# A two-layer macaron decoder trunk on one core: the same instructions ordered by the scheduler with another machine model

## The chip, the cores and the metric

The kernel runs on one NeuronCore of a Trainium2 chip. The metric is the device time of one execution in microseconds (us). Five engines work side by side, each through its own queue in order: TensorE (PE, matmuls), VectorE (DVE), ScalarE (ACT), GpSimd (POOL) and SyncE (SP, which issues nearly all transfers). An instruction waits at the head of its queue until the semaphores that it needs are up, and holds everything behind it.

## The reference

```python
def reference(x, mem, ...):
    mem_n = _rmsnorm(mem, mem_norm_g)
    h = x                                            # (1, 512, 1024) float32
    for l in range(DEPTH):                           # 2 layers
        f = _swiglu(_rmsnorm(h, ffn1_pre_g[l]), ffn1_w_gate[l], ffn1_w_up[l], ffn1_w_down[l])
        h = h + 0.5 * _rmsnorm(f, ffn1_post_g[l])
        u = _rmsnorm(h, mix_pre_g[l])
        proj = u @ w_in[l]                           # q, k, v of two attentions, forget logits, q of the memory
        o_sb = _stick_breaking_attention(...)        # 8 heads of 64
        o_fx = _forgetting_attention(...)            # 8 heads of 64
        o_mem = _memory_attention(...)               # 4 heads of 128, over 256 rows of mem_n
        g_sb, g_fx, g_mem = jnp.split(jax.nn.sigmoid(u @ w_gate[l] + b_gate[l]), 3, axis=-1)
        merged = (g_sb * (_merge_heads(o_sb) @ w_br_sb[l]) + g_fx * (_merge_heads(o_fx) @ w_br_fox[l])
                  + g_mem * (_merge_heads(o_mem) @ w_br_mem[l]))
        h = h + _rmsnorm(merged @ w_out[l], mix_post_g[l])
        f = _swiglu(_rmsnorm(h, ffn2_pre_g[l]), ffn2_w_gate[l], ffn2_w_up[l], ffn2_w_down[l])
        h = h + 0.5 * _rmsnorm(f, ffn2_post_g[l])
    return h
```

`_swiglu` is `(silu(t @ w_gate) * (t @ w_up)) @ w_down` with 1024 columns in and 2816 inside.

## The kernel before

The names end in a letter and the layer: the trunk is a0 (first feed-forward of layer 0), b0 (token mixing), c0 (second feed-forward), then a1, b1, c1. The activations lie turned, 128 columns of the model by 512 tokens a tile.

**Every float32 matmul is made of three.** A weight block comes in as `raw_...` (512 KB, one transfer issued on SP, L249 or, for the blocks of the feed-forwards, L297). ACT rounds it to the high part `wh_...` (a cast, L182, or L185 with a scale), DVE subtracts that from the raw block for the low part `wl_...` (L183, or L186). Activations are split likewise (`uh`/`ul`, `us`, `ah`/`al`). `mm3` then gives PE high by high (L205), a product with one low part (L206) and one with the other (L207). Which of the two is the weight's depends on the side that it stands on: in the products of the feed-forwards L206 reads `wl` and L207 reads the low part of the activations.

**Feed-forward.** Gate and up products of the first columns are made by seven products of half size over sums of blocks (numbered 0 to 6, traced in the order 0, 2, 1, 3, 4, 5, 6; `token_product`). Tiles are named `pw` + feed-forward + `g` or `u`, the group of columns, and the sum into which the product goes. The weight sums of products 2, 3, 5 and 6 are made on DVE (L327, in tiles `t...` and `raw_...`), the activation sums too (`x11`, `x10`, `x00`, L700 to L722), and are split into `uh.._n` and `ul.._n` for product n. The results go through ACT copies and Silu (L775, L781, L786) and DVE sums (L777). The down products (`pda`, `pdc`) follow, with gate and up columns that are left over between them.

**After a product's last tile**: `result` (ACT L535 squares and sums, DVE L540 scales), `rstd` (DVE L486, ACT L483 and L488, DVE L490 and L491) and the residual (DVE L558 for the last feed-forward, then the store).

**The memory.** `mem_stats` loads the 256 rows of mem in two tiles `mstat_0` and `mstat_1` (L1022), squares and sums them on ACT (L1024) and scales on DVE (L1025). `mem_norm` makes the reciprocal root of that: ACT Ln and Exp (L1036, L1037) and four small DVE operations (L1038 to L1041). They are used late in the first feed-forward.

**The start** (`begin`) loads four tiles of x, takes their root mean squares (L535, L483, L488, L490, L491), scales and turns them (`utx`) and splits them (`us_x`).

**What sets the order.** The kernel's own planner `Q` interleaves these jobs by estimated PE times, and so sets the order in which the instructions are traced. After that the scheduler of the tile framework places each instruction in its engine's queue: it goes through the traced instructions with a model of the machine, and takes those first that this model holds ready. Some are pinned: within the start (`in_order`) and with `keep_in_program_order` they keep their traced order on their engine. The call stands in `kernel`, where the context of the framework is opened.

## Time and profile before

| | us |
|---|---|
| median of three runs | 2379.33 (2377.66 to 2384.99) |
| the profiled execution | 2378.89 |
| its span, first to last instruction | 2377.2 |
| PE busy in the span | 2348.8 |
| DVE busy | 1805.5 |
| ACT busy | 1515.2 |
| POOL busy | 76.0 |

Times in the views are counted from the start of the span. Matmuls are pipelined and drawn longer than the distance of two, so a PE that is drawn busy can still lose a little. The granted clock of TensorE is 0.999 in the mean.

### The profile page before, as it was taken

What the parts mean: (1) busy time and instruction counts of PE and PEld (TensorE: products, weight loads), DVE (VectorE), ACT (ScalarE), POOL (GpSimd) and SP (SyncE); (2) the same over time, 40 slices, a digit from 0 to 9 for tenths busy, and PEclk for the clock granted to TensorE, in tenths of its full rate; (3) what the DMA queues carried; (4) which work ended last, traced back from release to release, by engine and by line L of the source; (5) the groups of instructions that cost most, each with busy time, mean ns of one, the idle gap of its engine ahead of it and who ended that gap; (6) DMA issues with size and microseconds to landing.
All of it is one profiled execution on the core that took longest, in us unless ns stands there. A gap on an engine that the chain in (4) does not pass through costs nothing.

```text
span 2377.2 us, 31155 instructions
## 1 busy us (share of the span) xinstructions
PE 2348.8 (99%) x11719; PEld 1982.8 (83%) x11719; DVE 1805.5 (76%) x2358; ACT 1515.2 (64%) x2306; POOL 76.0 (3%) x134
## 2 busy tenths in 40 slices
PE   9999999999999999999999999999999999999998
PEld 7777889888888888778888878888888888887787
DVE  8876877667777689778788778766777767897785
ACT  6777565577766556775557665655777664666744
POOL 0000000000111000000000000000001100000000
PEclk9999999999999999999999999999999999999999
DMA  5666455223223556664647664532323235576643
GB/s 199 194 176 182 159 190 151 75 81 94 86 75 107 186 178 177 185 186 142 230 134 208 182 177 161 199 110 71 98 72 98 80 116 200 160 203 171 194 145 141
DMA packets 299754, 354.98 MB, mean 149 GB/s; under 512 B 78266, under 2 KB 192978, under 8 KB 299604
## 3 DMA queue, kind: packets, MB, share of 16 engines
q1 hardware_dynamic: 299508, 352.97, 48.3%
q8 instruction: 92, 1.51, 0.3%
q14 instruction: 58, 0.48, 0.1%
q0 software_dynamic: 96, 0.03, 0.0%
HBM read 319.39 MB, written 16.78 MB: 141 GB/s over the span
## 4 chain that ended last, share of the span: by engine, by line
PE 84%; DVE 5%; DMA 5%; ACT 4%; issue 2%; SPq 0%; POOL 0%; DVEq 0%; ACTq 0%
PE pg L206 4%; PE pg L205 4%; PE pg L207 4%; PE pda L206 2%; PE pda L207 2%; PE pdc L206 2%; PE pda L205 2%; PE pdc L207 2%; PE pdc L205 2%; PE pb L207 1%; PE pb L206 1%; PE pb L205 1%; DMA raw_da<-in_ffn_w_down_dram 1%; PE pq L206 1%; PE pq L205 1%
## 5 line engine op out<-in xcount | busy, mean ns | idle before, releaser
L205 PE MATMUL pg<-us_a,wh_wg 128*128 128x512 f32 x384 | 150.9, 393 | 0.0
L207 PE MATMUL pg<-us_a,wl_wg 128*128 128x512 f32 x384 | 149.8, 390 | 0.0
L206 PE MATMUL pg<-us_a,wh_wg 128*128 128x512 f32 x384 | 149.8, 390 | 0.0
L206 PE MATMUL pda<-wl_da,aha 128*128 128x512 f32 x224 | 87.8, 392 | 3.5 <-DVE wl_da L183 3.5
L206 PE MATMUL pdc<-wl_dc,ahc 128*128 128x512 f32 x224 | 87.9, 392 | 3.0 <-DVE wl_dc L183 3.0
L205 PE MATMUL pdc<-wh_dc,ahc 128*128 128x512 f32 x224 | 86.8, 390 | 1.4 <-ACT wh_dc L182 1.3
L205 PE MATMUL pda<-wh_da,aha 128*128 128x512 f32 x224 | 86.7, 390 | 1.1 <-ACT wh_da L182 1.1
L207 PE MATMUL pdc<-wh_dc,alc 128*128 128x512 f32 x224 | 87.2, 389 | 0.0
L207 PE MATMUL pda<-wh_da,ala 128*128 128x512 f32 x224 | 87.2, 389 | 0.0
L183 DVE TENSOR_TENSOR wl_da<-raw_da,wh_da 128x1024 fp32r<-128x1024 f32 x50 | 60.9, 1223 | 34.3 <-ACT wh_da L182 34.3
L207 PEld LDWEIGHTS pg<-us_a,wl_wg 128*128 128x128 f32 x384 | 72.1, 188 | 15.2
L183 DVE TENSOR_TENSOR wl_dc<-raw_dc,wh_dc 128x1024 fp32r<-128x1024 f32 x50 | 61.0, 1222 | 30.5 <-ACT wh_dc L182 30.4
L205 PEld LDWEIGHTS pg<-us_a,wh_wg 128*128 128x128 f32 x384 | 72.1, 188 | 14.1
L206 PEld LDWEIGHTS pg<-us_a,wh_wg 128*128 128x128 f32 x384 | 72.2, 188 | 14.1
L182 ACT CAST wh_da<-raw_da 128x1024 fp32r<-128x1024 f32 x50 | 52.2, 1050 | 47.0 <-PE pda L207 16.6
L182 ACT CAST wh_dc<-raw_dc 128x1024 fp32r<-128x1024 f32 x50 | 52.3, 1050 | 43.5 <-PE pdc L207 17.6
L186 DVE SCALAR_TENSOR_TENSOR wl_wg<-raw_wg,wh_wg 128x1024 fp32r<-128x1024 f32 x48 | 58.4, 1220 | 22.2 <-ACT wh_wg L185 22.2
L200 DVE SCALAR_TENSOR_TENSOR ga<-pg,bgate,ga 128x512 f32<-128x512 f32 x48 | 35.9, 747 | 50.0 <-ACT ga L199 50.0
L185 ACT ACTIVATE wh_wg<-raw_wg 128x1024 fp32r<-128x1024 f32 x48 | 50.6, 1058 | 24.7 <-PE pv L1096 11.7
L183 DVE TENSOR_TENSOR wl_uc<-raw_uc,wh_uc 128x1024 fp32r<-128x1024 f32 x44 | 53.7, 1220 | 16.5 <-ACT wh_uc L182 16.5
L182 ACT CAST wh_uc<-raw_uc 128x1024 fp32r<-128x1024 f32 x44 | 46.1, 1050 | 30.7 <-PE pgc L206 7.6
L183 DVE TENSOR_TENSOR wl_ua<-raw_ua,wh_ua 128x1024 fp32r<-128x1024 f32 x44 | 53.6, 1219 | 15.0 <-ACT wh_ua L182 15.0
(647 smaller groups left out, 8053.7 us busy)
## 6 DMA issues: line engine op xcount, KB each, us to landing
raw_da<-in_ffn_w_down_dram SPq DMA_DIRECT2D x66, 512.0 KB, 4.4
raw_dc<-in_ffn_w_down_dram SPq DMA_DIRECT2D x66, 512.0 KB, 4.2
raw_ga<-in_ffn_w_gate_dram SPq DMA_DIRECT2D x52, 512.0 KB, 4.3
raw_ua<-in_ffn_w_up_dram SPq DMA_DIRECT2D x52, 512.0 KB, 4.4
raw_gc<-in_ffn_w_gate_dram SPq DMA_DIRECT2D x52, 512.0 KB, 4.1
raw_uc<-in_ffn_w_up_dram SPq DMA_DIRECT2D x52, 512.0 KB, 3.6
raw_wg<-in_w_gate_dram SPq DMA_DIRECT2D x48, 512.0 KB, 3.5
raw_wo<-in_w_out_dram SPq DMA_DIRECT2D x24, 512.0 KB, 3.4
```

What stands on the lines that cost most here:

```text
L182: both = [nc.scalar.copy(h_ap, src)]
L183: make = lambda: nc.vector.tensor_tensor(l_ap, src, h_ap.bitcast(F32), ALU.subtract)
L185: both = [nc.scalar.activation(h_ap, src, AF.Copy, scale=scale)]
L186: make = lambda: nc.vector.scalar_tensor_tensor(l_ap, src, scale, h_ap.bitcast(F32), ALU.mult, ALU.subtract)
L200: nc.vector.scalar_tensor_tensor(t, z, minus, t, ALU.max, ALU.add)
L205: nc.tensor.matmul(pt, lh, rh, start=start, stop=False, skip_group_check=free)
L206: nc.tensor.matmul(pt, lh, rl, start=False, stop=False, skip_group_check=free)
L207: nc.tensor.matmul(pt, ll, rh, start=False, stop=stop, skip_group_check=free)
```

## The change

One argument is added where the context is opened:

```diff
-    with tile.TileContext(nc) as tc:
+    with tile.TileContext(nc, schedule_with_timeline_sim=True) as tc:
         tile_macaron_trunk_kernel(tc, *args)
```

The traced instructions stay the same. The scheduler now orders them with the machine model that keeps a time line, in place of the plain one. Matmuls, DVE operations and transfers are the same in number; the loads of ACT's function tables, which follow from the order, are 12 instead of 15. The queues of all engines change: on DVE and ACT about every second row stands elsewhere, on PE a fifth of the matmuls move by more than 2 us' worth of matmuls and none by more than 20. Three places:

**ACT in the start, between the third and the fourth input tile** (`us_x` is the split input, `nhx` the root mean square's small tile, `mstat_808` the first tile of the memory, `mem_rstd` its statistics; - before, + now):

```order
 L185 ACTIVATE us_x_130<-utx_0_277 128x4x128
+L185 ACTIVATE us_x_131<-utx_1_284 128x4x128
 L483 ACTIVATE nhx_114<-nhx_114,eps_t 128x1
-L185 ACTIVATE us_x_131<-utx_1_284 128x4x128
+L1024 ACTIVATE mstat_808,mem_rstd<-mstat_808 128x1024
 L488 ACTIVATE nhx_114<-nhx_114 128x1
+L1036 ACTIVATE mem_rstd<-mem_rstd 128x1
+L1037 ACTIVATE mem_rstd<-mem_rstd 128x1
 L185 ACTIVATE us_x_130<-utx_0_322 128x4x128
```

The statistics of the memory, which came after the first Silu, now stand within the root mean square of the fourth input tile. On DVE, L1025 likewise stands ahead of that tile's L490, and on SP the transfer of `mstat_0` is issued as the 13th block of 512 KB instead of the 19th. The second tile's follow ahead of `wh_ga_0_2_0`, with three table loads more than before in the first 65 us.

**PE at the start of a0's down product, the end of its up product** (`pda` is the down product, `wh_da`/`wl_da` its first weight block, `pwa0u` the up product). Before:

```order
L207 MATMUL pwa0u_1_0_1_1431<-wh_ua0_1_5_2_1544,ula0_5_665 128x512
L205 MATMUL pda0_0_0_1742<-wh_da0_0_0_0_1623,aha0_0_0_1670 128x512
L206 MATMUL pda0_0_0_1742<-wl_da0_0_0_0_1624,aha0_0_0_1670 128x512
L207 MATMUL pda0_0_0_1742<-wh_da0_0_0_0_1623,ala0_0_0_1671 128x512
L205 MATMUL pda0_0_0_1742<-wh_da0_0_0_0_1623,aha0_0_0_1670 128x512
L205 MATMUL pwa0u_1_0_0_1430<-wh_ua0_1_6_0_1583,us_x_1_131 128x512
```

Now:

```order
L207 MATMUL pwa0u_1_0_1_1431<-wh_ua0_1_5_2_1544,ula0_5_665 128x512
L205 MATMUL pda0_0_0_1742<-wh_da0_0_0_0_1623,aha0_0_0_1670 128x512
L205 MATMUL pda0_0_1_1743<-wh_da0_0_0_0_1623,aha0_0_0_1670 128x512
L205 MATMUL pwa0u_1_0_0_1430<-wh_ua0_1_6_0_1583,us_x_1_131 128x512
L206 MATMUL pwa0u_1_0_0_1430<-wl_ua0_1_6_0_1584,us_x_1_131 128x512
...
L207 MATMUL pwa0u_1_0_0_1430<-wh_ua0_1_6_2_1588,us_x_1_131 128x512
L206 MATMUL pda0_0_0_1742<-wl_da0_0_0_0_1624,aha0_0_0_1670 128x512
```

Twelve matmuls of the up product now stand between the products with `wh_da` and the first one with `wl_da`.

**PE in the gate product of c0** (`pwc0g`; the numbers behind `wh_gc0_0_` are product and row of the block; a1 and c1 change alike). Before:

```order
L207 MATMUL pwc0g_0_0_1_8095<-wh_gc0_0_3_2_8131,ulc0_3_8104 128x512
L205 MATMUL pwc0g_0_2_0_8135<-wh_gc0_0_4_0_8166,uhc0_4_8185 128x512
L206 MATMUL pwc0g_0_2_0_8135<-wl_gc0_0_4_0_8167,uhc0_4_8185 128x512
...
L207 MATMUL pwc0g_0_2_1_8136<-wh_gc0_0_4_2_8170,ulc0_4_8186 128x512
L205 MATMUL pwc0g_0_0_0_8094<-wh_gc0_0_5_0_8211,uhc0_5_8236 128x512
L206 MATMUL pwc0g_0_0_0_8094<-wl_gc0_0_5_0_8212,uhc0_5_8236 128x512
```

Now:

```order
L207 MATMUL pwc0g_0_0_1_8095<-wh_gc0_0_3_2_8131,ulc0_3_8104 128x512
L205 MATMUL pwc0g_0_0_0_8094<-wh_gc0_0_5_0_8211,uhc0_5_8236 128x512
L205 MATMUL pwc0g_0_0_1_8095<-wh_gc0_0_5_0_8211,uhc0_5_8236 128x512
L206 MATMUL pwc0g_0_0_0_8094<-wl_gc0_0_5_0_8212,uhc0_5_8236 128x512
...
L205 MATMUL pwc0g_0_2_0_8135<-wh_gc0_0_4_0_8166,uhc0_4_8185 128x512
L206 MATMUL pwc0g_0_2_0_8135<-wl_gc0_0_4_0_8167,uhc0_4_8185 128x512
```

Product 5 now begins ahead of product 4, by the 24 matmuls that product 4 has.

On DVE, ahead of the `wl` of product 5's first block, the rows of L722 and of product 4's `ul` are gone and those of product 5's `ul` and of two L327 sums for product 6 have come; in the last tiles of c1, L540 and L486 of tile 3 stand ahead of L490, L491 and L558 of tile 2.

## The prediction

> **What bounds the kernel now.** I read the page's busy shares first, then its chain of waits, then the list of what PE waited for, then stretches of the span with PE, DVE and ACT side by side.
>
> ```profile
> PE 2348.8 (99%) x11719; PEld 1982.8 (83%) x11719; DVE 1805.5 (76%) x2358; ACT 1515.2 (64%) x2306; POOL 76.0 (3%) x134
> ...
> PE 84%; DVE 5%; DMA 5%; ACT 4%; issue 2%; SPq 0%; POOL 0%; DVEq 0%; ACTq 0%
> ```
>
> ```profile
> PE pda L206 <- DVE wl_da L183: 3.5, 4, 1.3
> PE pdc L206 <- DVE wl_dc L183: 3.0, 4, 0.8
> PE pwa0u L205 <- ACT wh_ga L182: 2.0, 1, 2.0
> PE warm L1565 <- DVE warm L1656: 1.3, 1, 1.3
> PE pdc L205 <- ACT wh_dc L182: 1.3, 1, 1.3
> PE pda L205 <- ACT wh_da L182: 1.1, 1, 1.1
> PE pwa0g L207 <- DVE ula L183: 1.1, 1, 1.1
> PE pwc1u L206 <- DVE wl_uc L183: 0.8, 1, 0.8
> PE pwa0u L206 <- DVE wl_ua L183: 0.8, 1, 0.8
> PE gqx L526 <- DMA grow<-in_ffn_pre_g_dram: 0.8, 1, 0.8
> PE pwa1u L206 <- DVE wl_ua L183: 0.6, 1, 0.6
> PE pwo L206 <- DVE wl_wo L183: 0.6, 1, 0.6
> ```
>
> PE is the bound nearly everywhere, and the change neither adds nor drops a matmul, so only PE's waits can move the end. The list (engine, line, what was waited for: us in all, times, the longest; the eleven rows of 0.6 us and less behind these are left out) is short: no wait in it is longer than 2.0 us. Most are of one kind: a matmul of the low part (L206, weight wl) stands at the head of PE's queue while DVE still makes that low part.
>
> A row understates a wait. In
>
> ```profile
> 903.56 0.39 PE L207 MATMUL pwc0g<-wh_gc,ulc 128*128 128x512 f32 x1
> 903.79 0.39 PE L205 MATMUL pwc0g<-wh_gc,uhc 128*128 128x512 f32 x1
> ...
> 909.23 0.39 PE L205 MATMUL pwc0g<-wh_gc,uhc 128*128 128x512 f32 x1
> ```
>
> a matmul is drawn 0.39 us long while the next starts 0.23 later, so an idle of x in the list costs x + 0.16.
>
> **The change part by part.** Terms are added to the profiled execution's 2378.9 us, which is 0.4 below the median of the three runs, 2379.3.
>
> *1. Waits that are filled.* Wherever PE waited for a wl or a DVE result, the new order sets matmuls whose operands are long there ahead of the waiting one. At the start of the down product (second place shown above) 12 matmuls stand between the L205 and the first L206: 12 x 0.23 = 2.7 us, where the wait was at most 1.3. The waits on wh_da and wh_dc stay, since the L205 still comes straight after the same ACT cast. In the list the fillable rows are the wl ones, the wh_ga one and the ula one: 12.4 us in 14 waits, hence 12.4 + 14 x 0.16 = 14.6 us. The ula wait (1.1 + 0.16) lies in the first feed-forward's start, counted under 3. That leaves **-13.4**. Bounds: -20, if nearly the whole list went, with its small rows, and -6.7, if half of the fillers wait themselves.
>
> *2. Product 5 ahead of product 4.* In the gate product of the last three feed-forwards (third place above) PE takes product 5 before product 4, that is 24 matmuls sooner: from 909.23 to 903.79, and its first L206 from 909.46 to about 904.3. DVE makes that wl here:
>
> ```profile
> 902.59 1.21 DVE L183 TENSOR_TENSOR ulc<-x11c,uhc 128x1024 fp32r<-128x1024 f32 x1
> 903.73 1.21 DVE L327 TENSOR_TENSOR raw_gc<-tgc,raw_gc 128x1024 f32<-128x1024 f32 x1
> 904.86 1.21 DVE L183 TENSOR_TENSOR wl_gc<-raw_gc,wh_gc 128x1024 fp32r<-128x1024 f32 x1
> 900.00:920.00 20.00, 20.00 (x89) 16.26 (x88) 19.82 (x20) 11.56 (x13) 0.00 (x0) 1.00 0.68 213
> ```
>
> The third row's wl ends at 906.1, one DVE operation every 1.13 us. In the new order two of the operations ahead of it go behind (L722 and the ulc of product 4) and three come ahead (the ulc of product 5 and two L327 sums), so it ends at 906.1 + 1.13 = 907.2. PE then waits 907.2 - 904.3 = 2.9 us at its head, with product 4 ready or nearly so behind it. The last row (columns: length, PE, PEld, DVE, ACT, POOL busy, clock, DMA share, GB/s) shows DVE busy 19.82 of 20 us: nothing gives the lag back in this stretch. Three places: **+8.7**. Bounds: 0, if the lag only replaces later waits, and 10.
>
> *3. The memory statistics move to the start.* ACT's Square of mem, which stood at 36.50, now stands between L483 and L488 of the fourth input tile, and DVE's L1025 ahead of the L490 that follows:
>
> ```profile
> 22.21 0.21 ACT L488 ACTIVATE nhx<-nhx 128x1 f32<-128x1 f32 x1
> 34.23 1.28 ACT L623 ACT_TABLE_LOAD   x1
> ...
> 36.50 1.06 ACT L1024 ACTIVATE mstat<-mstat 128x1024 f32<-128x1024 f32 x1
> 37.45 0.20 ACT L1024 ACTIVATION_READ_ACCUMULATOR mstat<-mstat 128x1 f32 x1
> 77.78 0.14 DVE L1025 TENSOR_SCALAR mem_rstd<-mem_rstd 128x1 f32<-128x1 f32 x1
> ...
> 95.75 0.21 DVE L1041 TENSOR_SCALAR mem_rstd<-mem_rstd 128x1 f32<-128x1 f32 x1
> 2.00:14.00 12.00, 11.07 (x33) 5.72 (x32) 5.16 (x13) 6.82 (x15) 0.95 (x3) 1.00 0.96 331
> 30.00:90.00 60.00, 58.90 (x293) 49.68 (x293) 59.50 (x68) 42.70 (x53) 0.00 (x0) 1.00 0.42 136
> ```
>
> The chain fourth tile, turn, us_x is longer by 1.06 + 0.20 = 1.25 us. Between 30 and 90 DVE is busy 59.5 of 60 us, so there it is DVE that sets the pace, and what is put into its queue is paid in full: the ten small mem_rstd operations of which first and last are shown came at 78 to 96 and now come before 65, 10 x 0.18 = 1.8. Three more table loads before 65, 3 x 1.28 = 3.8 us, fall into ACT's 17.3 idle us and cost nothing by themselves (without that cover, 3.8). The order in the first feed-forward's products 3 and 4 makes a wl some 2.4 us late, worked out as under 2. Sum 5.45, of which some 0.5 is covered by four product matmuls now ahead of the turn: **+5**. The transfer decides the bounds: mstat_0 is now the 13th transfer of 512 KB instead of the 19th, 6.8 MB up to its end; at the 331 GB/s of the stretch from 2 to 14 it lands at about 22.6, and ACT gets there at 22.2. Bounds 1 and 9.
>
> *4. The tail.* DVE's last tile now does L540 and L486 ahead of the third tile's L490, L491 and two L558:
>
> ```profile
> 2368.33 1.41 DVE L558 SCALAR_TENSOR_TENSOR hfc<-fc,nfc,hfc 128x512 f32<-128x512 f32 x2
> 2370.65 0.69 DVE L540 SCALAR_TENSOR_TENSOR fc<-pdc,gpc 128x512 f32<-128x512 f32 x1 [0.90 <-ACT sqc L535]
> 2371.26 0.20 DVE L486 TENSOR_SCALAR nfc<-nfc 128x1 f32<-128x1 f32 x1
> 2371.96 0.22 DVE L490 SCALAR_TENSOR_TENSOR nfc<-nfc 128x1 f32<-128x1 f32 x1 [0.50 <-ACT nfc L488]
> ```
>
> So 1.41 + 0.4 us of the third tile's work, which was done before the last matmul, falls between 2371.5 and the last L490; 0.5 of it fits into the wait for ACT: **+1.3**. Bounds 0 and 1.5.
>
> *5. Token mixing.* At six places (about 588, 643, 677, 1764, 1820, 1854) a transposed weight block is split on DVE behind a weight correction that it used to precede:
>
> ```profile
> 672.61 1.67 DVE L183 TENSOR_TENSOR ptf<-ptf,ptf 128x128 fp32r<-128x128 f32 x4
> 677.24 1.23 DVE L183 TENSOR_TENSOR wl_wb<-raw_wb,wh_wb 128x1024 fp32r<-128x1024 f32 x1 [2.96 <-ACT wh_wb L182]
> 678.49 0.68 DVE L186 SCALAR_TENSOR_TENSOR q<-pq,q 64x512 fp32r<-64x512 f32 x1
> ```
>
> There the split of ptf now follows the q of 678.49, so ends after 679.3, and PE reaches the pvf product that reads it at about 678.3. Worked out so, the six are 1.0 to 1.7 us late. Before, DVE sat idle 2.96 us at this point, so it catches up; I take half, 6 x 0.7 = **+4**. Bounds 0 and 8.
>
> SP's order changes too (the next block's loads go ahead of some down weights), but there the transfers had 10 us and more in hand: nothing, and 2 to 3 us per place if that cover were gone.
>
> Sum: -13.4 + 8.7 + 5 + 1.3 + 4 = +5.6, hence 2378.9 + 5.6 = 2384.5; with the 0.4 to the median, **2385 us**.
>
> **The rivals.** *A, the fills win.* The late wl of product 5 and of the start replace waits that come behind them, as a PE that is late finds its operands ready. For it: the waits of the down products lie behind each of these places on the same chain. Against: DVE at 19.82 of 20 us. Terms 2 and 3 shrink to 2 and 1.5, and 5 to 0: -13.4 + 2 + 1.5 + 1.3 = -8.6, about 2371.
>
> *B, the transfer holds ACT and DVE.* If mstat_0 shares the bandwidth with those issued just after it, 16 transfers, 8.4 MB, must come in: at 331 GB/s it lands near 27, some 5 us after ACT gets there, and us_x, hence all of PE after its few fillers, waits; DVE, the pace-setter until 90, loses as much. From 4 us late on this alone decides. 2385 + 5 = 2390.
>
> [...]
>
> *C, the fills fail.* The fillers need weights as young as the wl that they cover; if half of them wait, term 1 is -6.7: 2385 + 6.7, about 2392. For it: in the 900 to 920 stretch DVE has no slack to make anything earlier. Against: at the down products the fillers are a product whose weights lie ready.
>
> *That the order hardly changes* is excluded: about a fifth of all matmuls move by more than 2 us.
>
> **How the numbers follow.** Forecast 2385: 0.46, with its own range from 2377 to 2392. A (2371): 0.22. B (2390): 0.14. C (2392): 0.18. A measurement of this kernel can tell about 0.3%, 7.1 us, from no change, that is below 2372 or above 2386.5. Faster: most of A, since it has the lower bounds of term 1 below it, and a little of the forecast, 0.19. Within: over half of the forecast, 0.26, with 0.05 of A and 0.04 of B and C, 0.35. Slower: the rest, 0.46. The range from 2368 to 2399 leaves out 0.1 on either side; its ends answer to about -11 and +20, where the bounds of all terms at once would give -19 and +22.
>
> **What would show it.** Right: no L206 <- wl_da or wl_dc wait, three waits of 2 to 3.4 us of a pwc0g, pwa1g and pwc1g L206 on its wl; L488 of the fourth tile at about 23.5; the last L558 ending 1.3 us further behind the last L540. Wrong: a start in which us_x is more than 3 us late (B), new PE waits of 0.5 us and more on wl inside the down products (C), or product 5 without a wait (A). A PE wait above 3.5 us anywhere, or one on a DMA, would mean that I missed a step.

## The result, and the profile after

| | before | after |
|---|---|---|
| median, us | 2382.16 (2377.66 to 2386.56, 4 runs) | 2413.60 (2411.40 to 2415.33, 4 runs) |
| the profiled execution, us | 2378.89 | 2411.40 |
| its span, us | 2377.2 | 2409.7 |
| mean granted clock of TensorE | 0.999 | 0.993 |

The ratio is 1.0136, 95% interval 1.0123 to 1.0150: the change makes the kernel 31.4 us slower. The forecast was 2385, and its range ended at 2399.

The changed kernel's page, busy time by engine and the shares of the chain of waits:

```profile
PE 2364.3 (98%) x11719; PEld 1987.6 (82%) x11719; DVE 1801.8 (75%) x2358; ACT 1508.9 (63%) x2303; POOL 82.2 (3%) x134
...
PE 87%; DVE 6%; DMA 3%; ACT 3%; issue 2%; DVEq 0%; SPq 0%; ACTq 0%
```

Same work, PE drawn 15.5 us longer, and waits between. Its list of what PE waited for (us in all, times, the longest):

```profile
PE pts L1135 <- DVE k L183: 5.7, 2, 2.8
PE pv L205 <- DVE ga L200: 2.6, 2, 1.3
...
PE pwc0g L206 <- DVE wl_gc L183: 1.6, 1, 1.6
PE pb L205 <- ACT o L182: 1.6, 2, 0.8
PE pwa1g L205 <- ACT sa L775: 1.6, 1, 1.6
PE pwc1g L205 <- ACT sc L775: 1.6, 1, 1.6
PE pwc0g L205 <- ACT sc L775: 1.6, 1, 1.6
PE pwc1g L206 <- DVE wl_gc L183: 1.6, 1, 1.6
```

The rows on `wl_da` and `wl_dc`, which headed the list before, are gone. In their place stand `pts`, `pv` and `pb`, which lie in the token mixings and had no row there at all, and at the first gate product of c0, a1 and c1 two kinds of wait.

**Where the time went.** For every PE record I took the distance to the next one, less the usual distance of its form (0.227 us for 128x512), and summed what is left by stage. It is the time that PE loses to waits and to a lower clock together; in the kernel before it is 38.6 us in all, after it is 69.9. Differences to the kernel before, in us, with four of the experiments below beside them ("gate" is the first gate chunk):

| stage | after | three places, DVE put back (e13) | mixings put back (e17) | start put back (e18) | four stretches put back (e12) |
|---|---|---|---|---|---|
| a0, the first 80 us of PE's work | +4.0 | +3.8 | +4.0 | -0.1 | +0.3 |
| a0, the next 70 us | -2.4 | -2.5 | -1.9 | -1.6 | +0.4 |
| rest of a0 | -2.8 | -2.8 | -2.8 | -1.8 | -2.9 |
| token mixing b0 | +9.9 | +9.8 | +0.9 | +9.6 | +0.6 |
| gate of c0 | +6.7 | +0.3 | +6.4 | +7.0 | 0.0 |
| rest of c0 | -0.6 | -0.5 | +2.8 | +2.6 | -1.4 |
| gate of a1 | +4.3 | +0.2 | +4.3 | +4.3 | 0.0 |
| rest of a1 | -1.6 | -1.0 | +0.4 | +2.1 | -3.3 |
| token mixing b1 | +11.6 | +11.4 | +6.6 | +11.4 | +4.7 |
| gate of c1 | +5.4 | +0.6 | +5.7 | +5.3 | 0.0 |
| rest of c1 | -3.2 | -0.5 | -1.5 | -2.6 | -4.0 |
| sum | +31.3 | +18.8 | +24.9 | +36.2 | -5.6 |

Single stages scatter by 1 to 3 us from run to run, as one half-clock stretch more or less falls on them: the rest of c0 stands at +2.8 and +2.6 with e17 and e18, which have one at 1003 and at 1009 us, and at -0.6 with the changed kernel, whose clock is 1.00 there.

**The gate of c0.** PE between product 3 and product 5 (start, drawn length, instruction, in brackets the idle time and its releaser):

```profile
912.17 0.39 PE L207 MATMUL pwc0g<-wh_gc,ulc 128*128 128x512 f32 x1
914.18 0.98 PE L205 MATMUL pwc0g<-wh_gc,uhc 128*128 128x512 f32 x2 [1.62 <-ACT sc L775]
916.81 0.79 PE L206 MATMUL pwc0g<-wl_gc,uhc 128*128 128x512 f32 x1 [1.65 <-DVE wl_gc L183]
```

Product 5 adds into the banks that hold product 3's sum, and ACT must first copy that sum out (L775). Before, the 24 matmuls of product 4, which has other banks, lay over the copy. Now PE stands for it, 1.78 us, and again for `wl`, 1.91 us. The windows behind (length, busy time of PE, PEld, DVE, ACT, POOL, then the granted clock, DMA share, GB/s):

```profile
914.00:916.00 2.00, 0.98 (x2) 0.37 (x2) 2.00 (x3) 0.61 (x2) 0.00 (x0) 1.00 0.00 0
916.00:918.00 2.00, 1.19 (x3) 1.00 (x4) 2.00 (x3) 0.08 (x1) 0.00 (x0) 0.54 0.55 153
918.00:920.00 2.00, 2.00 (x7) 1.52 (x6) 2.00 (x2) 0.97 (x1) 0.00 (x0) 0.50 0.97 314
920.00:922.00 2.00, 2.00 (x6) 1.61 (x5) 0.23 (x1) 0.47 (x1) 0.00 (x0) 0.50 0.77 226
922.00:924.00 2.00, 2.00 (x8) 1.55 (x7) 1.23 (x1) 0.57 (x1) 0.00 (x0) 0.75 1.05 386
```

The clock falls to half and stays there for 2 x (0.46 + 0.50 + 0.50 + 0.25) = 3.4 us' worth of lost clock, 6.8 us of time, in which PE issues a matmul every 0.43 us. And DVE (L722 and the last row make product 4's factor):

```profile
910.99 1.22 DVE L183 TENSOR_TENSOR ulc<-x00c,uhc 128x1024 fp32r<-128x1024 f32 x1
912.12 1.22 DVE L327 TENSOR_TENSOR tgc<-raw_gc,tgc 128x1024 f32<-128x1024 f32 x1
913.26 1.22 DVE L183 TENSOR_TENSOR wl_gc<-raw_gc,wh_gc 128x1024 fp32r<-128x1024 f32 x1
914.39 1.22 DVE L327 TENSOR_TENSOR tgc<-raw_gc,tgc 128x1024 f32<-128x1024 f32 x1
915.53 1.22 DVE L183 TENSOR_TENSOR wl_gc<-raw_gc,wh_gc 128x1024 fp32r<-128x1024 f32 x1
916.66 1.22 DVE L722 TENSOR_TENSOR x11c<-x11c,us_b 128x1024 f32<-128x1024 f32 x1
...
919.00 1.22 DVE L183 TENSOR_TENSOR ulc<-x11c,uhc 128x1024 fp32r<-128x1024 f32 x1
```

Four of the five rows above L722 (all but 913.26) belong to products 5 and 6, and two L327 sums for product 5 ran further up: six instructions of 1.14 us that the plain order has behind L722. Product 4's low part ends at 920.2 here, at 903.8 in the kernel before, where PE reaches this gate 8.6 us sooner (its first `pgc0` matmul at 856.7 instead of 865.3): against PE it is 8 us later.

**The token mixing b0.** PE, DVE and ACT around 588 us (`ts` is the stick-breaking chain of a head, `pts` its turned weights):

```profile
592.11 1.76 PE L1135 MATMUL pts<-ident,ts 128*128 128x128 f32 x7 [2.83 <-DVE k L183]
...
588.12 0.95 DVE L1173 TENSOR_TENSOR_SCAN ts<-cut,ts 128x384 f32<-128x384 f32 x1
588.99 1.20 DVE L183 TENSOR_TENSOR wl_wb<-raw_wb,wh_wb 128x1024 fp32r<-128x1024 f32 x1
590.22 0.69 DVE L186 SCALAR_TENSOR_TENSOR q<-pq,q 64x512 fp32r<-64x512 f32 x1
590.94 0.56 DVE L1174 TENSOR_TENSOR ts<-zs,ts 128x384 f32<-128x384 f32 x1
591.53 0.52 ACT L1175 ACTIVATE ts<-ts 128x384 f32<-128x384 f32 x1 [0.28 <-DVE ts L1174]
```

The list puts this wait down to `k`, which ended last, at 592.08; but the matmuls of L1135 read `ts`, and its last step on ACT (L1175) ended at 592.05, as late. Between the chain's scan and its last step on DVE stand the low part of a weight that is used later, and a `q`. In the kernel before that last L1174 ran ahead of both:

```profile
585.13 0.55 DVE L1174 TENSOR_TENSOR ts<-zs,ts 128x384 f32<-128x384 f32 x1
585.62 1.23 DVE L183 TENSOR_TENSOR wl_wb<-raw_wb,wh_wb 128x1024 fp32r<-128x1024 f32 x1
```

### The profile page after: what moved, and what is told of

It reads as the page before. It is cut to its first block, busy times and chain, and to the rows that moved or that the text cites. A ratio compares the mean times of both kernels' runs of the same rounds, so it can differ in the third digit from the quotient of the medians.

```text
span 2409.7 us, 31116 instructions
## 1 busy us (share of the span) xinstructions
PE 2364.3 (98%) x11719; PEld 1987.6 (82%) x11719; DVE 1801.8 (75%) x2358; ACT 1508.9 (63%) x2303; POOL 82.2 (3%) x134
## 4 chain that ended last, share of the span: by engine, by line
PE 87%; DVE 6%; DMA 3%; ACT 3%; issue 2%; DVEq 0%; SPq 0%; ACTq 0%
PE pg L206 4%; PE pg L205 4%; PE pg L207 3%; PE pda L205 3%; PE pda L207 3%; PE pda L206 3%; PE pdc L205 3%; PE pdc L207 2%; PE pdc L206 2%; PE pb L205 2%; PE pb L206 2%; PE pb L207 2%; PE pwo L205 1%; PE pwo L207 1%; PE pwo L206 1%
## 5 line engine op out<-in xcount | busy, mean ns | idle before, releaser
L206 PE MATMUL pg<-us_a,wh_wg 128*128 128x512 f32 x384 | 151.6, 395 | 0.0
L206 PE MATMUL pda<-wl_da,aha 128*128 128x512 f32 x224 | 87.2, 389 | 0.0
L206 PE MATMUL pdc<-wl_dc,ahc 128*128 128x512 f32 x224 | 87.1, 389 | 0.0
L205 PEld LDWEIGHTS pg<-us_a,wh_wg 128*128 128x128 f32 x384 | 72.8, 190 | 14.8
L206 PEld LDWEIGHTS pg<-us_a,wh_wg 128*128 128x128 f32 x384 | 72.7, 189 | 14.4
L182 ACT CAST wh_ua<-raw_ua 128x1024 fp32r<-128x1024 f32 x44 | 45.9, 1049 | 20.9 <-PE pwa1u L207 6.4
```

The lines of the kernel that those rows point to most:

```text
L182: both = [nc.scalar.copy(h_ap, src)]
L205: nc.tensor.matmul(pt, lh, rh, start=start, stop=False, skip_group_check=free)
L206: nc.tensor.matmul(pt, lh, rl, start=False, stop=False, skip_group_check=free)
```

## The experiments

All ratios are against the kernel before, timed beside it on the same chip, so they are to be held against the change's 1.0136.

### e1: product 4 ahead of product 5 again, on PE alone

```diff
-                        mm3(pts[e][:], h[:, kk, c], l[:, kk, c], un.h[:, k], un.l[:, k], opens and kk == 0,
+                        with (tc.issue_after(st["end", 4]) if n == 5 else nullcontext()): mm3(pts[e][:], h[:, kk, c], l[:, kk, c], un.h[:, k], un.l[:, k], opens and kk == 0,
                             ends and kk == ND // 2 - 1, free=True)
-                        yield 3 * S * PE_US
+                        st["end", n] = nc.cur_bb.bb.instructions[-1]; yield 3 * S * PE_US
```

> The changed kernel with one thing added: in every token product, product 5's matmuls are issued behind product 4's, as the plain scheduler had them; nearly all else stays where the time-line model put it. Theory A (product 5 directly behind product 3 waits for the scalar engine's copy of product 3's sum, L775, out of the banks into which it adds, then for its own wl, and the clock halves after the two waits): the waits at 912, 1256 and 2108 us go, with the half-clock stretches at 917, 1260 and 2114; the three places cost 16.4 us over the back-to-back issue, so the kernel takes 2396 to 2401 us. Theory B (the vector engine is simply late there, whichever product comes next, as the prediction had it: 2.9 us at each place): product 4 waits in place of product 5, and the time stays at 2408 to 2414 us.

Measured: 2431.88 us, ratio 1.0192 (1.0174 to 1.0210), worse than the change itself. Both theories miss it. Its waits:

```profile
PE pwc0g L205 <- ACT uhc L182: 7.0, 1, 7.0
PE pwc1g L205 <- ACT uhc L182: 6.3, 1, 6.3
PE pwa1g L205 <- ACT uha L182: 5.4, 1, 5.4
```

Product 4 is not "ready or nearly so", as the prediction had it: its factor is 5 to 7 us away, because DVE still does the later products' work first. Taking product 5 first was the better answer to a DVE order that was wrong already.

### e2: PE kept busy in the waits

```diff
+            with tc.issue_after(st["end", 3]):
+                for k in range(7+nb): nc.tensor.matmul(st["c", 2][0][:], zero[:], x[:, k % 4, 0, :], start=False, stop=False, skip_group_check=True)
```

Seven of them are held ahead of product 5's first matmul, the others (7, in a1 3) ahead of its first L206: 14 more matmuls in c0 and c1, 10 in a1.

> The changed kernel with 17 to 14 matmuls of zero weights added on TensorE at each of the three places where product 5 waits (c0, a1, c1): 7 behind product 3, and 7 (a1: 3) behind product 5's first two matmuls. They add nothing to the sums and stand in the time of the waits. Theory A (the half-clock stretches behind these waits, 2.6, 1.6 and 1.4 us lost, come from TensorE standing still in them): with the engine kept busy the granted clock stays at 1.00 at the three places, the waits themselves stay, and the kernel takes 2407 to 2410 us, 4 to 6 us less than the changed one. Theory B (the clock falls for another reason, such as the time of the program): the half-clock stretches stay and the time is 2413 to 2418 us.

Measured: 2414.61 us, ratio 1.0121 (1.0097 to 1.0144); mean clock 0.996 instead of 0.993. The same stretch of c0:

```profile
917.41 1.77 PE L1707 MATMUL pwc0g<-us_b,zero 128*128 128x512 f32 x7
919.50 0.50 PE L206 MATMUL pwc0g<-wl_gc,uhc 128*128 128x512 f32 x1 [0.31 <-DVE wl_gc L183]
...
918.00:920.00 2.00, 1.69 (x8) 1.10 (x7) 2.00 (x3) 0.00 (x0) 0.00 (x0) 1.00 0.29 40
920.00:922.00 2.00, 2.00 (x10) 1.60 (x10) 2.00 (x3) 1.05 (x1) 0.00 (x0) 1.00 0.93 318
```

On the clock theory A holds: at all three places it stays at 1.00, with product 5 waiting for `wl` as before. On the time it isn't shown: the interval takes in 4 us less as well as no change, since half-clock stretches came elsewhere instead (1011 and 2209 us).

### e3: the stick-breaking chain of one head ahead of the splits

```diff
-        both.append(make())
+        with (tc.issue_after(tsl["ts"]) if "ts" in tsl else nullcontext()): both.append(make())
...
-            nc.vector.tensor_tensor(t[:, :w], zr, t[:, :w], ALU.subtract)
+            sub = nc.vector.tensor_tensor(t[:, :w], zr, t[:, :w], ALU.subtract).ins; tsl.update({"ts": sub} if name.endswith("_2_1") else {})
```

> The changed kernel with one thing added: the stick-breaking chain of head 2_1 in both token mixings is put ahead of the splits (weight and query halves) that were traced behind it, on the vector and the scalar engine alone, until that head's sum over the values is traced. Theory A (TensorE's waits at 588 and 1784 us on pts come from the vector engine doing weight halves ahead of that chain, L1168, L1173, L1174, and the half-clock stretches behind them follow from the wait): both go, 6.2 and 5.9 us, and the kernel takes 2399 to 2404 us. Theory B (the chain is late from its start, since the products before it end late): the wait stays at 2 us or more at both places, and the time at 2409 to 2414 us.

Measured: 2415.00 us, ratio 1.0122 (1.0104 to 1.0140). The wait on `pts` fell from 3.6 to 1.5 us at both places and the half-clock stretch behind it went, 3.6 and 4.9 us by the sums over PE. But a `pv` matmul 66 us later now waited 1.5 us, with 0.2 or 0.3 behind it, and the time didn't move by more than it can be measured. The chain's place makes that wait; repairing one head hands part of it on.

### e8: the swap alone, in the kernel before

The plain scheduler, with product 4 held behind product 5 on PE in the gates of c0, a1 and c1:

```diff
+            for i in st["four"]:
+                tc.add_manual_dep(i, own[-1].name, nosync, reason="swapped")
```

> The kernel before, with its plain scheduler, and one part of the change alone: in the first gate chunk of c0, a1 and c1 product 4's matmuls are issued behind the whole of product 5. Theory A (the swap itself costs the copy's wait, the wl wait and the clock): 16 us in all, 2394 to 2400 us, with half-clock stretches behind the waits. Theory B (the prediction's price, 2.9 us for wl at each of three places and no copy to wait for): 2386 to 2392 us. Theory C (the swap is harmless and the loss has to do with the vector engine's new order): 2379 to 2384 us.

Measured: 2395.88 us, ratio 1.0041 (1.0018 to 1.0063), 9.3 us more than the kernel before on the same chip (2386.63). That difference is B's in size, though the interval is wide (4 to 15 us); in its pieces it is A's, a wait for the copy and in c0 a half-clock stretch. In c0:

```profile
904.38 0.99 PE L205 MATMUL pwc0g<-wh_gc,uhc 128*128 128x512 f32 x2 [0.58 <-ACT sc L775]
905.98 0.73 PE L206 MATMUL pwc0g<-wl_gc,uhc 128*128 128x512 f32 x2 [0.60 <-DVE wl_gc L183]
907.12 0.57 PE L207 MATMUL pwc0g<-wh_gc,ulc 128*128 128x512 f32 x1 [0.40 <-DVE ulc L183]
```

The three places cost 4.3, 2.7 and 2.7 us by the sums over PE, 9.7 in all. With DVE in the plain order the swap costs about what the prediction said, 8.7, but not for its reason: the wait for `wl` costs 0.8 and not 2.9, with 0.7 for the copy and 0.6 for `ul` beside it. The other 6.7 of the change's 16.4 are left for the other orders of DVE and ACT.

### e7: six instructions on DVE put behind L722

The corrections and splits traced behind the factor of product 4 are issued behind it in c0, a1 and c1; PE is not touched.

```diff
-                ins = nc.vector.tensor_tensor(src, a, b, ALU.subtract)
+                with (tc.issue_after(tsl["ts"]) if "ts" in tsl else nullcontext()): ins = nc.vector.tensor_tensor(src, a, b, ALU.subtract)
...
-            pair(4, s)
+            pair(4, s); tsl.update({"ts": nc.cur_bb.bb.instructions[-1]} if name != "a0" else {})
```

> The changed kernel with one edit, on the vector engine alone: in b's end to c0, in c0 to a1 and in c1 the corrections and low halves that belong to products 5 and 6 are issued behind the low half of product 4's factor (L722 and its L183), as the plain scheduler had them; on TensorE nothing is pinned, and the scheduler by itself puts product 4 ahead of product 5 again. Theory A (the swap on TensorE is only an answer to the vector engine's order: six instructions of 1.14 us for later products are issued ahead of L722, which made product 4 wait 7.2, 5.5 and 6.5 us when product 5 was held back alone): no wait over 1 us at the three places, no half-clock stretch there, 16 us less than the changed kernel, a ratio to the kernel before of 1.006 to 1.008. Theory B (the vector engine has more to do there than fits, in any order): a wait of 3 us or more moves to product 5 or 6, and the ratio stays over 1.011.

PE's order went back by itself, as expected: product 4 first, and no wait at products 4 and 5. Yet the time was 2415.14 us, ratio 1.0115 (1.0084 to 1.0147). The losses came back one product on, 5.3, 2.7 and 5.7 us, at the start of the up chunk:

```profile
928.89 0.73 PE L205 MATMUL pwc0u<-wh_uc,us_b 128*128 128x512 f32 x2 [0.83 <-ACT wh_uc L182]
931.78 0.69 PE L206 MATMUL pwc0u<-wl_uc,us_b 128*128 128x512 f32 x1 [2.15 <-DVE wl_uc L183]
...
927.10 1.22 DVE L327 TENSOR_TENSOR tuc<-tuc,raw_uc 128x1024 f32<-128x1024 f32 x1
...
929.37 1.22 DVE L327 TENSOR_TENSOR tuc<-tuc,raw_uc 128x1024 f32<-128x1024 f32 x1
930.50 1.22 DVE L183 TENSOR_TENSOR wl_uc<-raw_uc,wh_uc 128x1024 fp32r<-128x1024 f32 x1
```

It is the same fault again: two sums for up product 2 stand ahead of the `wl` of up product 0, which PE needs next. In the kernel before the `wl` comes first.

### e4: the memory statistics alone

```diff
-            nc.scalar.activation(raw[:], raw[:], AF.Square, accum_out=ss[:, 0:1])
+            tc.keep_in_program_order(nc.scalar.activation(raw[:], raw[:], AF.Square, accum_out=ss[:, 0:1]))
```

and the same for L1036.

> The changed kernel with one edit: the squares of the memory statistics (L1024) and their logarithms (L1036) are kept in the program's order, which puts them behind the start, as in the kernel before. Theory A (the prediction's third term: they cost the first token products 5 us by the table loads and by the scalar engine's time): 3.6 us less than the changed kernel, a ratio of 1.011 to 1.013, and the half-clock stretch at 63 us gone. Theory B (the start is late for another reason): the same ratio as the changed kernel, 1.0136, and the same waits at 47, 59 and 63 us.

Measured: 2420.10 us, ratio 1.0134 (1.0105 to 1.0162); the interval takes in both theories. The half-clock stretch at 63 us went, as A has it; the waits at 47 and 59 us stayed, the second half as long (1.0 us instead of 2.0). The first 80 us got 1.0 us shorter, and the next 70 us lost 5.6: a wait of 3.2 us for `wh_ga` came at 114 us, where the kernel before has one of 2.1, with a half-clock stretch behind it. The early statistics cost the start something, 1.0 of its 4.0 us, and pay it back there.

### e10, e11, e12, e13: stretches put back in the plain scheduler's order

From here on chosen engines are chained, for chosen stretches, in the order that they have in the kernel before; everything else is left to the time-line model. The lists of instruction numbers are long, the edit is short:

```diff
-        tile_macaron_trunk_kernel(tc, *args)
+        tile_macaron_trunk_kernel(tc, *args); as_before(nc, tc)
...
+    for numbers in AS_BEFORE:
+        chain = [by[f"I-{n}"] for n in numbers if f"I-{n}" in by]
+        for a, b in zip(chain, chain[1:]):
+            tc.add_manual_dep(b, a.name, nosync, reason="as_before")
```

> The changed kernel with the vector, scalar and GpSimd engines' order put back as the plain scheduler had it, in the two token mixings alone (the work that ran from 556 to 842 and from 1751 to 2037 us in the kernel before); TensorE's order is left to the scheduler. Theory A (the mixing's 21 us, of which the wait on pts is only a part, all come from the order of these engines): waits on pv, pts, pb and pvf go with their half-clock stretches, some 20 us less than the changed kernel, a ratio of 1.004 to 1.007. Theory B (part of it is due to TensorE's order or comes from outside the stretch): a ratio of 1.008 to 1.012.

e10 measured: 2411.42 us, ratio 1.0100 (1.0071 to 1.0128): B. The waits on `pts`, `pb` and `pvf` went, with the half-clock stretches behind them 16 us by the sums over PE; the one on `pv`, at the head of the stretch, stayed, and new ones came where the stretch ends: 2.4 us at `pgc0`, 3.5 at `utb1`.

> The changed kernel with the vector, scalar and GpSimd engines' order put back as the plain scheduler had it in the four stretches where the changed kernel lost (the start to 75 us, both token mixings with what leads into them and the factors of c0 and c1 behind them, and the end of c0 with a1's factor), and the memory statistics put back to where they were; the weight preparation in the chunks and in the down products stays as the time-line model ordered it. Theory A (losses and gains are separate, so that the gains of 14.8 us at the fills can be had alone): 2366 to 2374 us where the kernel before takes 2382, a ratio of 0.994 to 0.997. Theory B (the gains depend on what the time-line model did earlier, for instance on transfers started sooner): a ratio of 1.000 or more.

e11 measured: 2392.49 us, ratio 1.0022 (1.0006 to 1.0038). That is B by the number. Most of the loss is gone, and nothing gained: there are waits at the seams again, `utb` 2.6 and 1.7 us, `pwa0u` 2.2, and one of 2.9 us for `wh_ga` at 115 us, behind the memory statistics. Ahead of `utb` PE, which was left free, ran 16 matmuls of c0's gate among the last output products, so these ended later, and with them the chain that turns the last tile.

> The changed kernel with the vector engine alone put back to the plain scheduler's order, from the transposes ahead of c0's, a1's and c1's first gate chunk to the middle of their first up chunk (868 to 960, 1205 to 1310 and 2062 to 2155 us of the kernel before); scalar engine and TensorE are left to the scheduler. The run with six instructions moved showed the wait gone at product 5 and come back one chunk on, at the first product of the up chunk (2.5 to 3.3 us), where two corrections (tuc, L327) ran ahead of the low half that product needs. Theory A (each such wait is made by the vector engine doing later products' corrections before the halves needed next, so that the plain order on this engine alone is enough): no wait over 1.2 us at any of the three places or in the up chunk behind them, no half-clock stretch there, 14 to 17 us less than the changed kernel, a ratio of 1.006 to 1.008. Theory B (the vector engine is behind with its work as a whole, so any order only moves the wait on): the waits come again further on and the ratio stays at 1.011 to 1.014.

e13 measured: 2402.95 us, ratio 1.0064 (1.0046 to 1.0083): A. The three gates are back at +0.3, +0.2 and +0.6 us with nothing touched but DVE, and the largest wait in the first up chunks behind them is 0.75 us. This settles the gates.

> The changed kernel with TensorE, vector, scalar and GpSimd engines put back to the plain scheduler's order in four stretches (0 to 135, 545 to 960, 1195 to 1310 and 1740 to 2155 us of the kernel before); the rest, with most of the weight preparation at the chunks' ends and in the down products, is left to the time-line model. Theory A (losses and gains are separate, and what was left of the losses in the run before this one came from TensorE's order, which was free there, and from the ends of the stretches): 2368 to 2375 us where the kernel before takes 2382, a ratio of 0.994 to 0.997. Theory B (a place where the order changes from one model's to the other's makes a wait of its own, of 2 to 4 us): a ratio of 0.998 to 1.003.

e12 measured: 2376.54 us (2372.31 to 2379.84, 6 runs) against 2385.61, ratio 0.9955 (0.9938 to 0.9972), 9 us faster than the kernel before: A. Its longest waits:

```profile
PE pwa0u L205 <- ACT wh_ga L182: 2.5, 1, 2.5
PE pts L1135 <- ACT ts L1175: 2.5, 1, 2.5
```

The first is the old one behind the memory statistics, the second a seam at the head of b1. So losses and gains can be had apart. Whether it takes TensorE's order or other places for the seams, in which e11 differs, was not tried singly.

### e15: the fills alone

> All four engines in the plain scheduler's order but for four short stretches around the first down products of each feed-forward (185 to 240, 1020 to 1075, 1360 to 1410 and 2200 to 2245 us of the kernel before), which are left to the time-line model: the fills alone, the prediction's first term. The kernel before waits there 3.1, 3.3, 2.5 and 2.0 us. Theory A (the time-line model fills these waits by itself, whatever stands ahead): 6 to 9 us less than the kernel before, a ratio of 0.996 to 0.9975. Theory B (the fills were bought by work that it moved ahead of the stretch): a ratio of 0.999 to 1.001.

Measured: 2384.21 us, ratio 0.9994 (0.9981 to 1.0007): B. The waits at the first down products did get shorter, but others came, the largest 3.6 us for L1042, which scales the rows of mem. Fills that cost nothing elsewhere weren't to be had this way.

### e16: the vector engine's whole order

> The changed kernel with the vector engine's whole order put back to the plain scheduler's, all 2325 rows of it; TensorE, scalar, GpSimd and SyncE are left to the time-line model. Theory A (the vector engine's order makes all the losses and most of the gains; the other engines' orders follow from it): the ratio is 1.000, within 0.002, with waits at the down products' starts as in the kernel before. Theory B (TensorE's own order under this model makes waits too, as at the transposes behind the token mixings, 2.4 to 3.5 us, when vector and scalar engine were put back there alone): a ratio of 1.003 to 1.008. Theory C (the gains are TensorE's and the scalar engine's): a ratio of 0.994 to 0.997.

Measured: 2456.51 us, ratio 1.0293 (1.0266 to 1.0321): 70 us slower, outside all three theories, B's in kind. DVE has row for row the order that it has in the kernel before. Its three longest waits:

```profile
PE utb L578 <- DVE fb L568: 7.6, 2, 3.8
PE pda L205 <- ACT pda L827: 5.9, 2, 3.7
PE pts L1135 <- DVE fl L1341: 5.2, 2, 2.6
```

Over the whole program, a good order on one engine with other orders beside it was worse than a poor one that all share; in the three short stretches of e13 it was better.

### e17 and e18: a whole stretch on all four engines

> The changed kernel with all four engines put back to the plain scheduler's order from the end of a's last down product to the transposes behind the token mixing, in both layers (545 to 880 and 1740 to 2075 us of the kernel before). Put back on the vector, scalar and GpSimd engines alone, the waits on pts, pb and pvf had gone and new ones of 2.4 to 3.5 us had come at pgc0 and utb, where TensorE's order was free. Theory A (the mixing's own loss is 20 us, and a stretch put back on all engines keeps it): 17 to 21 us less than the changed kernel, a ratio of 1.005 to 1.007. Theory B (the waits at the stretch's end come with any seam between the two orders): a ratio of 1.009 to 1.012.

e17 measured: 2405.20 us, ratio 1.0078 (1.0057 to 1.0099), between the two. b0 came down to +0.9 us; b1 to +6.6, of which 4.3 are two waits at its head (`pv` 1.5, `pts` 2.8).

> The changed kernel with all four engines put back to the plain scheduler's order from the start to 135 us of the kernel before, and so with the memory statistics at 77 to 95 us again. Theory A (the prediction's third term, 5 us lost at the start): 3 to 5 us less than the changed kernel, a ratio of 1.0115 to 1.0125. Theory B (the statistics cost the same wherever they stand: the kernel before waits 2.1 us at 111 us for what they held up, and the run with the statistics moved alone showed 3.2 us at 114): the changed kernel's ratio, 1.013 to 1.014.

e18 measured: 2415.35 us, ratio 1.0119 (1.0101 to 1.0136). The start came down from +4.0 to -0.1, and 0.8 of the 2.4 gained in the 70 us behind it was given back; the interval takes in both theories, the sums of this stage speak for A. The whole sum is larger than the change's all the same (+36.2), since two half-clock stretches, at 1009 and 1354 us, fell on this execution that the changed kernel's did not have.

## Why the prediction was wrong

The direction was the one held likeliest, slower; the size was not. Of the 25.8 us between the forecast's +5.6 and the measured +31.4, term 5 holds 17.5 and term 2 holds 7.7. Behind both, the clock was put at nothing: no term has a share for it, but the trace before has a half-clock stretch behind two short waits, at 2170 us (last section).

**1, fills, -13.4: right in size.** No wait on `wl_da` or `wl_dc` is left, and the places where PE lost less sum to -14.8. But 2.2 of them, the `wh_ga` wait at 111 us, are no fill: e4 and e18 bring that wait back with the statistics. Some 1.6 more are that half-clock stretch at 2170 us, which went with the waits ahead of it and which the term did not count. And the fills don't come alone (e15).

**2, product 5 ahead of product 4, +8.7: 16.4 measured.** The step that failed is "PE then waits 907.2 - 904.3 = 2.9 us at its head, with product 4 ready or nearly so behind it". The wait for `wl` was 1.91, 0.82 and 1.84 us, less than forecast. What was left out is the wait for the copy of product 3's sum, 1.78 at each place, and the half clock behind the two, 2.6, 1.6 and 1.4 us (the clock that is lost while PE works). Under it lies a wrong reading: the swap was taken for the cause, when it was the scheduler's answer (e7: it went back by itself) to a DVE order that makes product 4's factor 8 us later. The rows for that were on the table, since L722 was seen to go behind; only product 5's `wl` was followed, not what L722 feeds. e1, e7 and e13 show it from three sides.

**3, the start, +5: +4.0, in part by luck.** L488 of the fourth tile ran at 23.93 (forecast 23.5), and the load of `mstat` was 0.98 us late for ACT:

```profile
22.87 1.06 ACT L1024 ACTIVATE mstat<-mstat 128x1024 f32<-128x1024 f32 x1 [0.98 <-DMA mstat<-in_mem_dram]
...
23.93 0.19 ACT L488 ACTIVATE nhx<-nhx 128x1 f32<-128x1 f32 x1
```

So rival B's transfer was late, but by 1 us and not 5. The sum is not made of the forecast's pieces, though: 1.6 of the 4.0 is a half-clock stretch at 63 us that the term did not have, behind waits of 1.1 us for `wh_ga` and 2.0 for `wl_ga`, and with the statistics alone put back only 1.0 went (e4). That the rest lies in the order of the start is shown by e18; in which rows is not. The term also left out the other side, 2.4 us gained in the 70 us behind it.

**4, the tail, +1.3: right.** From the last matmul to the end of the span it is 8.4 us, before 7.3; the last L558 ends 4.35 us after the last L540 starts, before 3.17.

**5, token mixing, +4: 21.5 measured, the largest miss.** The step that failed is the choice of places: they were sought by one kind of moved row, the split of `ptf` behind a weight correction, and of its six places two show a wait (`pvf`, 0.6 us each). The chain of L1168, L1173 and L1174 in front of `pts` (3.6 us at each mixing), the `ga` in front of `pv` (1.5) and the `o` in front of `pb` (1.0) moved in the same way and were not followed. "DVE sat idle 2.96 us at this point, so it catches up" held for DVE and did PE no good, since the wait comes before the idle time. That these losses lie in the mixing's own order is shown for b0 by e17 (+9.9 to +0.9) and less cleanly for b1. Which engine's order makes them was not separated: e10 chains three engines, e17 four.

**The rivals.** A had the fills right and the places wrong. C fell: the fills held. The prediction's sign for a missed step, a wait over 3.5 us, came just short in the `pts` waits, 3.0 us with 0.6 ahead of them.

Still open is why the time-line model orders so. What the rows share is that work whose operands lay ready (the sums of later products) went ahead of work that is needed sooner but becomes ready a moment later; its own estimates were not looked at. SyncE's order of transfers was never put back; e12 shows that the losses go without it.

## What to carry to other kernels

Where an order changes, follow on each engine the first row that went behind, and ask what it feeds; a swap on the engine that sets the pace may be only the answer to it. A product that adds into a bank which another engine still has to read needs other work between, as product 4 was here: without it PE stood 1.78 us at each of the three places. And orders of several queues are one thing: with four stretches put back on all four engines the kernel was 9 us faster than before, with one engine put back over the whole program 70 us slower, and with that engine put back in three short stretches (e13) about half of the loss was gone.

## What was not expected of the hardware

The granted clock of TensorE fell to 0.50 behind short waits: in c0 behind two of 1.62 and 1.65 us with two matmuls between them, in e8 behind three of 0.58, 0.60 and 0.40 within 3 us (idle times as the views draw them). The kernel before had shown it already, behind 0.50 and 0.76 us; in the last row the granted clock is the 0.50:

```profile
2167.95 0.50 PE L205 MATMUL pwc1u<-wh_uc,us_b 128*128 128x512 f32 x1 [0.50 <-ACT wh_uc L182]
2169.21 0.50 PE L206 MATMUL pwc1u<-wl_uc,us_b 128*128 128x512 f32 x1 [0.76 <-DVE wl_uc L183]
2170.00:2172.00 2.00, 2.00 (x5) 1.59 (x6) 1.49 (x2) 1.06 (x1) 0.00 (x0) 0.50 0.82 232
```

**The length of a wait alone did not tell whether the clock fell.** Behind the 0.50 and 0.76 us above it fell. Behind the 1.97 us for `wh_ga` at 111 us in the kernel before it stayed at 1.00, and in e12, with 2.5 us at the same place, it stayed at 1.00 too. What decides between them is not shown here. In the traces before and after, the half-clock stretches last 3.41 or 6.83 us, but for the one that each program's end cuts off.

With 10 to 14 matmuls of zero weights in the waits the clock stayed at 1.00 at all three places (e2), where it fell to 0.50 in the changed kernel. In the changed kernel's profiled execution about 11 us are lost in such stretches, before 1.4, so nearly 10 of the 31 us lie in them. That all of these would be saved by keeping PE busy is not shown, since in e2 other stretches came.
